# Second layer's entry: x times the norm's weights and root before the split, its input products on scaled fp16 parts

## The chip, the cores and the metric

The kernel runs on one core of one Trainium2 chip. The metric is device time in microseconds (us) of one execution; the runs of the kernel before took 2181.03, 2181.20 and 2181.38 us. The engines are TensorE (PE in the profile, its weight loads PEld), VectorE (DVE), ScalarE (ACT), GpSimd (POOL) and SyncE (SP); DMA transfers are issued from SP and POOL.

## The reference, cut to what matters

An encoder of two layers over 1024 tokens with 1024 channels. Each layer enters with

```
h = rmsnorm(x, g_mix[l]);  p = h @ w_in[l]
c_q  = rmsnorm(p[:, :384], g_q[l])        # -> q = c_q @ w_uq
c_kv = rmsnorm(p[:, 384:640], g_kv[l])    # -> k, v = c_kv @ w_ukv
k_rope = rope(p[:, 640:672])
a, gt = split(p[:, 672:])
u = silu(layernorm(dwconv31(a * sigmoid(gt))))
x = x + concat(attention(q, k, v), u) @ w_o[l]
h2 = rmsnorm(x, g_ffn[l]);  z = dwconv3(h2 @ w_up[l])
x = x + (silu(zg) * zv) @ w_down[l]
```

rmsnorm(x, g) is x · 1/sqrt(mean x² + 1e-6) · g. The output is the rmsnorm of the last x with g_final. All data are float32.

## The kernel before, in words

**Layout.** Channels lie on the 128 partitions, tokens along the free dimension: x is eight tiles of 128 x 1024, called x_0 to x_7. A float32 product is made of three products of parts: a tensor is split into an upper part ("h", rounded) and a lower part ("l", what the rounding left), and h·h, h·l and l·h are added in PSUM. Most products of the kernel use fp16 parts that have been scaled by a power of two so that they lie well in fp16's range. The products of w_in, in both layers, use parts of the type fp32r instead, which need no scaling.

**Blocks.** w_in comes in 13 blocks of 128 columns and one of 64: g0 to g3 (the gate gt), a0 to a3, kv0 and kv1, kr (k_rope), q0 to q2. One block's product, here called a section, is 8 channel tiles x 2 halves of the tokens x 3 products of parts, which is 48 matmuls of 128x512; kr is 32. Its result fills two PSUM banks as one 128x1024 tile (pg, pa, pkv, pkr, pq).

**Order.** Every engine has its own list of instructions, and runs it in the order in which the program writes it (`manual_schedule`); an instruction that has to wait holds up all that stand behind it on its engine. In the feed-forward part (`feed`, with `wo_steps`, `up_steps` and `down_steps`) the list is made by `put(step, rank, f)`: a step is one product on PE, and f is emitted with that step, sorted by rank. In `project` a clock of costs in the code spreads the work of the vector engines over the sections.

**The end of layer 1** (`down_steps`, loop l = 0). The down product runs in seven passes (`ORDER` 1, 5, 6, 3, 7, 2, 4) over 11 pairs of channel tiles. Its fp16 inputs are called ab (activations, split on ACT at L1540 and DVE at L1541) and wd (weights, fetched by SP, scaled and split on ACT at L1493 and DVE at L1494). After a pass `evict` adds its PSUM banks (pd) to four x tiles: L1456 on DVE. Pass 4 is the last. Its last three steps run bank by bank (m = 0 to 3), so that its banks for x_4, x_5, x_6 and x_7, second half of the tokens, close one after another; the four evictions of it finish x.

**The norm of layer 2.** `norm_sums` squares x on ACT (L258, xsq) and adds the squares on DVE (L263, L265, xss). `norm_root` transposes the sums on PE (L284, rx_0t and rx_512t, for the first and the second half of the tokens) and takes the root in eight small DVE instructions (L295 to L303). `norm_spread` brings the root to all partitions on PE (L322), and ACT copies it (L1720, rx). For half 0 all of this lies within pass 4. `norm_apply` (L1722) multiplies x by the norm's weights g_mix in two instructions for each x tile and half: ACT makes the upper part xs_h (L1732), DVE the lower part xs_l (L1733, three operands); it also stores raw x to DRAM (the residual, x_mid). The root is not in xs: it multiplies the results later.

**Entry to layer 2** (`next_sections`, L534). `resume` has POOL fetch the blocks g0, a0 and g1 as fp32r (L204); `complete` then negates each on ACT (L208) and has POOL fetch it a second time with an adding DMA (L209), so the lower part needs no DVE. PE runs the three sections for half 0 (L558, L564), then for half 1; the root's transposes for half 1 stand behind g0's half 1, and its spread behind a0's half 1.

**The rest of the products** (`project`, from L876 on). The sections a1 to q2 follow (L245, kr at L810), then the keys k0 to k3, and u, n and v, which belong to the queries and values. The evictions bring the root in: a gate takes three instructions (DVE L649, ACT sigmoid L650, DVE L652), its glu one on DVE (L657), a latent (kv and q) one on DVE (L679), then a square on ACT and its addition on DVE, the rotary key an ACT copy and two on DVE (L718 to L721). Between them DVE and POOL work off the taps of the 31-tap convolution (DVE L2039; ACT L2045 makes "far" ones, which a DMA adds in). `root` and `rooted` normalize the latents; the parts of the normalized ones, kvs and cqs, feed the keys and queries (L748 ACT, L750 DVE).

**Buffers.** Tiles come from rings: `wr` has 3 slots of 128x1024 float32 (raw weights, far taps), `ws` 8, `m` 8, and `b` 31 (`blk`).

Of the kernel before, what the change touches and what calls it, by code (L numbers as in the profile page):

```python
# [18 lines left out]
T = 1024  # L19
D = 1024  # L20
DEPTH = 2
# [102 lines left out]
WARM = 8  # L124

# [19 lines left out]
class Encoder:  # L145
# [45 lines left out]
    def cast(self, l, name, tag="ws"):  # L191
        src = self.weight_source(l, name)
        if name != "kr":
            return self.cast_tile(src, f"w{name}{l}", tag)
        w = self.tmp(tag, f"w{name}{l}", F32R, (128, 8, 128))
        hi, lo = w[:, :, 0:64], w[:, :, 64:128]
        src = src.rearrange("p (k m) -> p k m", k=8)
        self.nc.gpsimd.dma_start(out=hi, in_=src)
        return w, hi, lo, src

    def cast_tile(self, src, name, tag="ws"):
        hi, lo = (self.tmp(tag, name + i, F32R, tuple(src.shape)) for i in "hl")
        w = hi, lo
        self.nc.gpsimd.dma_start(out=hi, in_=src)  # L204
        return w, hi, lo, src

# [196 lines left out]
    def run(self):  # L403
        nc, a = self.nc, self.a
        self.par = [self.cp.tile([128, NPAR], F32, name="par0")]
        self.first = self.blk("first")
        nc.scalar.dma_start(out=self.first[:, 0:520], in_=a["x_first"])
        self.ones_r = self.cp.tile([128, 128], F32R, name="ones_r")
        self.ones = self.ones_r.bitcast(F32)
        self.ones_b = self.ones_r.bitcast(BF16)[:, 1::2]  # L410
        nc.vector.memset(self.ones, 1.0)
# [3 lines left out]
        self.xd = [a["x"], self.dp.tile([8, 128, T], F32, name="x_mid")]  # L415
        carry = None
# [117 lines left out]
    def next_sections(self, l, nxt, supply):  # L534
        names = ("g0", "a0", "g1")
        w = [self.complete(*e) for e in nxt["w"]]
        for k in range(8):
            self.norm_apply(l, nxt["x"], nxt, 1, k)
        self.norm_sums(l, nxt["x"], nxt, 1, range(4, 8))
        supply(-16.0)  # L540
        self.pp.tile([128, T], F32, name=f"skip{l}", tag="w1", bufs=1)
        ps = [self.wide(f"p{n}{l}") for n in names]
        for c in range(2):
# [23 lines left out]
    def project(self, l, carry):  # L567
# [13 lines left out]
        col = lambda i, n=1: qk[:, i:i + n]  # L581
        st = {}
# [64 lines left out]
        def gate(j):  # L647
            g = gates[j] = self.blk(f"gate{l}_{j}")
            nc.vector.tensor_tensor(out=g, in0=ps[f"g{j}"], in1=rx, op=ALU.mult)  # L649
            nc.scalar.activation(out=g, in_=g, func=AF.Sigmoid)  # L650
            yield 1.22, 1.5
            nc.vector.tensor_tensor(out=g, in0=g, in1=rx, op=ALU.mult)  # L652
            yield 1.22, 0.0

        def glu(j):
            g = u[j] = gates.pop(j)
            nc.vector.tensor_tensor(out=g, in0=ps[f"a{j}"], in1=g, op=ALU.mult)  # L657
# [19 lines left out]
        def latent(name, out, key, j):  # L677
            c = self.blk(f"c{name}{l}")
            nc.vector.tensor_tensor(out=c, in0=ps[name], in1=rx, op=ALU.mult)  # L679
            out.append(c)  # L680
            if j == 0:
                st[key] = self.blk(f"{key}{l}")
                nc.scalar.activation(out=st[key], in_=c, func=AF.Square)
                yield 1.22, 0.0
# [3 lines left out]
            yield 1.22, 1.5  # L688
# [26 lines left out]
        def key_rope():  # L715
            p, cos, sin = ps["kr"], st["cos"], st["sin"]
            t = self.blk(f"krt{l}")
            nc.scalar.copy(out=t[0:64, :], in_=p[64:128, :])  # L718
            yield 0.0, 1.5
            nc.vector.tensor_tensor(out=t[0:64, :], in0=p[0:64, :], in1=t[0:64, :], op=ALU.add)  # L720
            nc.vector.tensor_tensor(out=t[0:64, :], in0=t[0:64, :], in1=rx[0:64, :], op=ALU.mult)  # L721
# [91 lines left out]
        def inputs(name):  # L813
            return lambda: self.product(ps[name], self.tiled(w[name]), hl)
# [60 lines left out]

        def supply(now, turn=TURN):  # L876
# [3 lines left out]
            while turning and turning[0][1] <= now + turn:  # L880
                name, at, e = turning.pop(0)
                w[name] = self.complete(*e)
# [10 lines left out]
        for n, (name, weight, emit, evict, after) in enumerate(seq):  # L893
            supply(clock["pe"])
# [282 lines left out]
    def up_steps(self, l, steps, put):  # L1177
# [7 lines left out]
        self.ds = self.cp.tile([128, 2 * NF], F32, name=f"ds{l}", tag="ds", bufs=1)  # L1185
# [239 lines left out]
        for f in range(NF):  # L1425
# [14 lines left out]
            put(c + max(STORE_LAG, SQUARE_LAG.get(f, 1)), 3, lambda f=f: act_store(f))  # L1440
        for j in range(NF // 2):
# [8 lines left out]
    def down_steps(self, l, steps, put):  # L1450
        nc, a = self.nc, self.a
        base, last, half = len(steps), l == DEPTH - 1, NF // 2
        done, rest = HALVES
        act, x, casts, w, pairs, ps, nxt, sq, late_r, turns, st = {}, {}, {}, {}, {}, {}, {}, {}, {}, {}, {}
# [43 lines left out]
        def total():  # L1498
            st["ps"] = self.pp.tile([128, 2 * NF], F32, name=f"ds{l}p", tag="d4", bufs=1)
            nc.tensor.matmul(st["ps"], self.ones, self.ds[:, 0:2 * NF], start=True, stop=True)  # L1500

        def scales():
            f = self.ds[:, 0:16]
            cut = lambda i, n=1: f[:, i:i + n]
            nc.vector.tensor_reduce(out=cut(0, 2), in_=st.pop("ps").rearrange("p (e f) -> p e f", e=2), op=ALU.add, axis=AX.X)
# [7 lines left out]
            st["a"], st["w"], st["up"], st["back"], st["nback"] = (cut(i) for i in (4, 5, 8, 9, 10))  # L1513

# [54 lines left out]
        def evict(i, m):  # L1569
# [4 lines left out]
            else:  # L1574
                plus(xm, ps[BANK_SET[i], m], st["nback" if o else "back"])

# [26 lines left out]
        put(base + DOWN_TOTAL, 0.6, scales)  # L1603
        for m in range(4):
# [40 lines left out]
        put(end - 1, 6, resume)  # L1645
# [75 lines left out]

    def norm_apply(self, l, x, nxt, c, k, cs=None, r=None):  # L1722
# [3 lines left out]
        if l < DEPTH:  # L1726
            g = self.par[l][:, P_GMIX + k:P_GMIX + k + 1]
            if c == 0:
                nxt["hl"].append([self.tmp("m", f"xs{l}_{k}{i}", F32R) if k >= 4 else self.blk(f"xs{l}_{k}{i}", F32R)
                                  for i in "hl"])  # L1730
            hi, lo = (t[:, cs] for t in nxt["hl"][k])
            nc.scalar.activation(out=hi, in_=xk, func=AF.Copy, scale=g)  # L1732
            nc.vector.scalar_tensor_tensor(out=lo, in0=xk, scalar=g, in1=hi.bitcast(F32),  # L1733
                                           op0=ALU.mult, op1=ALU.subtract)
            nc.sync.dma_start(out=self.xd[l][k][:, cs], in_=xk)
# [45 lines left out]
    def attention(self, l, u, conv, away, spill, kvs, loaded, ahead, wo, begun):  # L1781
# [119 lines left out]
        def sums(h, main, st, y, rb):  # L1901
            pr = self.bank(f"sr{l}_{h}", (8, 128))
            nc.tensor.transpose(pr, st["sums"], self.ident)
            rs = self.cp.tile([8, 128], F32, name=f"rs{l}_{h}", tag="rs", bufs=2)
# [299 lines left out]
```

## Time and profile before

| | us |
|---|---|
| median of three runs | 2181.2 |
| profiled execution, span | 2179.0 |
| around the span (median less span) | 2.2 |
| PE busy | 2169.7 |
| DVE busy | 1844.7 |
| ACT busy | 1456.6 |
| POOL busy | 537.2 |

The profile is one execution, recorded by the hardware; its span runs from the first to the last instruction. Times in the rows are in us from the start of the span, durations in ns where they are whole numbers above 100. A row of the chain of waits says when a stretch of work began, how long it took, on which engine and line. An arrow shows out<-in, and x48 is a count. An instruction's duration reaches past the start of the next one on the same engine, so that in a row of equal instructions the distance of their starts is what each costs its engine: eight DVE instructions of 0.75 us in a row start 0.66 us apart.

The program enters layer 2's products at 1087.24 us and begins layer 2's last value products, which feed attention, at 1276.99 us.

### The profile page before, as it was taken

The numbers are of one execution on the slowest core, as the hardware profiler recorded it, in microseconds if no ns is written. First come the engines' busy times: TensorE is split into PE (matmuls) and PEld (weight loads), VectorE is DVE, ScalarE is ACT, GpSimd is POOL, SyncE is SP. The second block draws the span as 40 slices with busy tenths as digits, with TensorE's granted clock in tenths as the row PEclk, the third lists the DMA queues.
The fourth block names the chain that finished last, engine by engine and source line by source line (L and its number), as shares of the span: only waits on it lengthen the run. The fifth ranks groups of instructions, "written<-read, shape, count | busy, mean of one in ns | idle before, by whom it ended". The sixth has DMA issues, their size and how long they took to land.

```text
span 2179.0 us, 29766 instructions
## 1 busy us (share of the span) xinstructions
PE 2169.7 (100%) x10722; PEld 1260.7 (58%) x10722; DVE 1844.7 (85%) x2531; ACT 1456.6 (67%) x2183; POOL 537.2 (25%) x534
## 2 busy tenths in 40 slices
PE   9999999999999999999999999999999999999998
PEld 8887665754444444644488876667544444446445
DVE  6989999879998887887859789998898888878877
ACT  6455888746898886554623668886478888865544
POOL 1223777211111111000012355771112111110000
PEclk9999999999999999999999999999999999999999
DMA  6898878754688885554578986886646888856533
GB/s 195 184 187 212 164 152 171 245 163 104 149 244 259 222 261 145 193 178 151 166 177 164 188 207 134 159 186 200 175 100 164 261 241 242 241 141 218 182 111 122
DMA packets 163013, 400.96 MB, mean 184 GB/s; under 512 B 21888, under 2 KB 29936, under 8 KB 162864
## 3 DMA queue, kind: packets, MB, share of 16 engines
q0 software_dynamic: 62528, 145.89, 36.4%
q1 hardware_dynamic: 100048, 252.63, 33.8%
q8 instruction: 84, 1.38, 0.3%
q10 hardware_dynamic: 288, 0.53, 0.1%
q14 instruction: 65, 0.53, 0.1%
HBM read 270.75 MB, written 69.66 MB: 156 GB/s over the span
## 4 chain that ended last, share of the span: by engine, by line
PE 98%; ACT 1%; DVE 1%; issue 0%; DMA 0%; DVEq 0%; ACTq 0%
PE p L1306 36%; PE pd L1551 18%; PE po L1026 7%; PE s L1818 7%; PE t L1858 5%; PE pq L245 3%; PE pa L245 3%; PE o L1880 2%; PE pkv L245 2%; PE pg L245 2%; PE pg L564 2%; PE pn L245 2%; PE o L1885 1%; PE pv L1794 1%; PE pk L245 1%; PE pa L564 1%
## 5 line engine op out<-in xcount | busy, mean ns | idle before, releaser
L1306 PE MATMUL p<-b,w 128*128 128x512 f16 x3696 | 800.0, 379 | 0.2
L1306 PEld LDWEIGHTS <-w 128*128 128x128 f16 x3696 | 358.7, 98 | 431.9 <-issue 0.8
L1551 PE MATMUL pd<-ab,wd 128*128 128x512 f16 (+2 forms) x1920 | 404.2, 373 | 0.0
L1196 POOL DMA_DIRECT2D wu<-in_w_up x176 | 152.2, 879 | 770.2 <-DVE w L1270 581.5
L1551 PEld LDWEIGHTS <-wd 128*128 128x128 f16 x1656 | 161.9, 98 | 179.4 <-issue 0.5
L1818 PE MATMUL s<-k,q 96*128 96x512 f16 x768 | 186.9, 379 | 0.0
L1270 DVE SCALAR_TENSOR_TENSOR w<-wu,wf,w 128x512 f16<-128x512 f32 (+1 forms) x216 | 177.2, 834 | 3.6 <-ACT w L1267 3.6
L1861 DVE SCALAR_TENSOR_TENSOR pt<-t,pt 128x512 f16<-128x512 f32 x256 | 163.0, 676 | 10.0 <-ACT pt L1860 9.0
L1267 ACT ACTIVATE w<-wu,wf 128x512 f16<-128x512 f32 (+1 forms) x216 | 164.8, 781 | 0.1
L1860 ACT ACTIVATE pt<-t 128x512 f16<-128x512 f32 x256 | 139.1, 596 | 32.0 <-PE t L1858 30.0
L1820 DVE TENSOR_REDUCE mx<-s 128x1 f32<-128x1024 f32 x128 | 155.0, 1211 | 1.0 <-PE s L1818 1.0
L1540 ACT ACTIVATE ab<-ac,ds 128x512 f16<-128x512 f32 x108 | 75.5, 717 | 108.7 <-DVE ac L1455 73.0
L1828 ACT ACTIVATE p<-s,mx 128x1024 f32<-128x1024 f32 x128 | 143.3, 1120 | 2.2 <-DVE mx L1820 1.8
L2039 DVE SCALAR_TENSOR_TENSOR conv<-gate,par,conv 128x1009 f32<-128x1009 f32 (+14 forms) x110 | 139.9, 1274 | 3.1 <-ACT conv L659 0.4
L2056 POOL TENSOR_SCALAR late<-gate,par 128x1019 f32<-128x1019 f32 (+13 forms) x99 | 135.5, 1368 | 27.2 <-PE pn L245 13.9
L1858 PE MATMUL t<-ident,p 128*128 128x128 f32 x1024 | 136.6, 275 | 0.9 <-ACT p L1828 0.6
L1858 PEld LDWEIGHTS t<-ident,p 128*128 128x128 f32 x1024 | 116.8, 141 | 34.8 <-issue 7.4
L1766 DVE SCALAR_TENSOR_TENSOR o<-zg,par,o 128x1023 f32<-128x1023 f32 x88 | 112.7, 1281 | 8.9 <-ACT o L1760 7.4
L1314 DVE SCALAR_TENSOR_TENSOR zg<-p,wf,zg 128x512 f32<-128x512 f32 x72 | 54.0, 750 | 71.2 <-PE p L1306 61.6
L1766 DVE SCALAR_TENSOR_TENSOR v<-zv,par,v 128x1023 f32<-128x1023 f32 x88 | 112.1, 1276 | 0.0
L1818 PEld LDWEIGHTS <-q 96*128 96x128 f16 x768 | 74.0, 97 | 64.6 <-issue 2.1
L1541 DVE SCALAR_TENSOR_TENSOR ab<-ac,ds,ab 128x512 f16<-128x512 f32 x108 | 79.9, 748 | 19.2 <-ACT ab L1540 19.2
(2179 smaller groups left out, 3814.1 us busy)
## 6 DMA issues: line engine op xcount, KB each, us to landing
wu<-in_w_up SPq DMA_DIRECT2D x98, 512.0 KB
wu<-in_w_up POOLq DMA_DIRECT2D x176, 256.0 KB, 4.8
sd<-in_w_down SPq DMA_DIRECT2D x44, 512.0 KB
ws<-sd SPq DMA_DIRECT2D x44, 512.0 KB
act<-v SPq DMA_DIRECT2D x36, 512.0 KB
ac<-act SPq DMA_DIRECT2D x72, 256.0 KB
wo<-in_w_o POOLq DMA_DIRECT2D x32, 256.0 KB, 7.7
x_mix<-y SPq DMA_DIRECT2D x32, 256.0 KB
```

The costliest lines, as they stand in the source:

```text
L245: nc.tensor.matmul(ps[:, HALVES[c]], w, x[:, HALVES[c]], start=(k == 0 and s == 0), stop=(k == n - 1 and s == 2))
L1026: self.nc.tensor.matmul(ps, p[:, sl], q[:, cs], start=(k == 0 and t == 0), stop=(k == 3 and t == 2))
L1196: nc.gpsimd.dma_start(out=dst, in_=src, accum_op=ALU.add)
L1267: nc.scalar.activation(out=t, in_=src, func=AF.Copy, scale=scale[f])
L1270: nc.vector.scalar_tensor_tensor(out=t, in0=src, scalar=scale[f], in1=hi, op0=ALU.mult, op1=ALU.subtract)
L1306: nc.tensor.matmul(ps, w[p][:, k * 128:(k + 1) * 128], b[:, q], start=(i in (1, 5, 2) and k == 0 and t == 0), stop=(k == 3 and t == 2), sk ...
L1551: nc.tensor.matmul(ps[t, m][:, cs], w[i, j][p][:, m * 128:(m + 1) * 128], b[:, q, cs], start=(i in (1, 5, 2) and j == 0 and s == 0), stop= ...
L1766: self.nc.vector.scalar_tensor_tensor(out=o[:, a:b], in0=z[:, at + a:at + b], scalar=self.par[l][:, tap:tap + 1], in1=o[:, a:b], op0=ALU.m ...
L1818: nc.tensor.matmul(ps[:, cs], q[0:96, i, qs], k[0:96, j, cs], start=(s == 0), stop=(s == 2))
L1820: nc.vector.tensor_reduce(out=mx, in_=ps, op=ALU.max, axis=AX.X, negate=True)
L1858: nc.tensor.transpose(tp[:, i, qi * 128:(qi + 1) * 128], st["p"][2 * qp + qi][:, kt * 128:(kt + 1) * 128], self.ident)
L1861: nc.vector.scalar_tensor_tensor(out=lo, in0=tp, scalar=P_SCALE, in1=hi, op0=ALU.mult, op1=ALU.subtract)
```

## The change

**In the up stage of layer 1**: 14 blocks of layer 2's w_in are loaded by SP (`next_load`) and squared on ACT (`next_squares`), which also sums the squares; the squares' sum is only needed for a scale. `total` and `scales` in the down stage carry these sums along, and `next_scales` (seven small DVE instructions) makes powers of two out of them: one for the weights, one for x, one for the way back. They stand in a new tile `wz`.

**At the entry to layer 2**: each block is fetched once, raw, by SP into a `wr` slot (`cast`); ACT makes its scaled fp16 upper part (`scaled`) and DVE its lower part (`scaled_rest`, 128x1024). This holds for g0, a0 and g1 at the end of the down stage (`split_next`) and for the later blocks in `supply`.

**x**: `norm_apply` multiplies x in place by wz (g_mix and the scale) and the root on DVE (L1828), casts the upper part to fp16 on ACT (L1829), and DVE subtracts it for the lower part (L1817, one x tile later). x_mid is stored from `evict` instead. The root of the second half therefore has to be there before the second half is multiplied: its transposes now stand behind the fifth of g0's eight channel tiles of half 0, its spread behind the fifth of a0's, and `norm_apply` of half 1 follows.

**Evictions in layer 2**: the root is in x already, so a gate is one ACT sigmoid with a scale, the glu one DVE instruction with a scale, a latent one ACT instruction (L706), the rotary key's copy is scaled and one DVE instruction less. The ring `rs` of the attention's sums has one slot instead of two.

```diff
@@ next_sections
-        w = [self.complete(*e) for e in nxt["w"]]
-        for k in range(8):
-            self.norm_apply(l, nxt["x"], nxt, 1, k)
-        self.norm_sums(l, nxt["x"], nxt, 1, range(4, 8))
-        supply(-16.0)
+        supply(-30.0)
+        w = [e[0] for e in nxt["ready"]]
+        self.norm_sums(l, nxt["x"], nxt, 1, (7,))
...
-                if (c, i) == (0, 0):
-                    self.upper_first(ps[i], self.tiled(w[i]), nxt["hl"], HALVES[c])
-                for k in range(8 if c or i else 0):
-                    self.partial(ps[i], self.tiled(w[i]), nxt["hl"], k, (c,))
-                if c == 1 and i == 0:
-                    self.norm_root(l, nxt, 1, self.bank)
-                if c == 1 and i == 1:
-                    self.norm_spread(l, nxt, 1, self.bank)
-        return nxt["hl"], nxt["r"], dict(zip(names, ps))
+                for k in range(8):
+                    self.partial(ps[i], tiles[i], nxt["hl"], k, (c,))
+                    if (c, i, k) == (0, 0, 4):
+                        self.norm_root(l, nxt, 1, self.bank)
+                    if (c, i, k) == (0, 1, 4):
+                        self.norm_spread(l, nxt, 1, self.bank)
+                        for m in range(8):
+                            self.norm_apply(l, nxt["x"], nxt, 1, m)
+        supply(-16.0)
+        return nxt["hl"], None, dict(zip(names, ps))
@@ scaled, scaled_rest
+        nc.scalar.activation(out=hi, in_=src, func=AF.Copy, scale=self.wz[:, 12:13])
...
+        self.nc.vector.scalar_tensor_tensor(out=lo, in0=src, scalar=self.wz[:, 12:13], in1=hi, op0=ALU.mult, op1=ALU.subtract)
@@ latent
-            nc.vector.tensor_tensor(out=c, in0=ps[name], in1=rx, op=ALU.mult)
+            if l:
+                nc.scalar.activation(out=c, in_=ps[name], func=AF.Copy, scale=by)
+            else:
+                nc.vector.tensor_tensor(out=c, in0=ps[name], in1=rx, op=ALU.mult)
@@ supply
+                if l and name in BLOCKS:
+                    e = self.scaled(*e)
+                    w[name] = e[0]
+                    launch(rest_of(e), st.get("n", -3) - 2)
+                    continue
@@ up_steps
+            for n in range(len(BLOCKS)):
+                m = at[NEXT_SQUARES] + 3 * n // 2
+                put(m - 6, 5.6, lambda n=n: next_load(n))
+                put(m, 2.7, lambda n=n: next_squares(n))
@@ down_steps
+            put(base + DOWN_TOTAL + 12, 6, next_scales)
+            for m in range(3):
+                put(at[4, tail] + m + 1, 1.5, lambda m=m: sums(1, (4 + m,)))
...
-                nxt["w"] = [self.cast(l + 1, n) for n in ("g0", "a0", "g1")]
+                nxt["raw"] = [self.cast(l + 1, n) for n in ("g0", "a0", "g1")]
...
+        put(end - 8, 6, resume)
+        for i in range(0 if last else 3):
+            put(end - 4 + i, 3.2, lambda i=i: split_next(i))
+            put(end - 3 + i, 3.6, lambda i=i: self.scaled_rest(*nxt["ready"][i]))
@@ norm_apply, l < DEPTH
-            nc.scalar.activation(out=hi, in_=xk, func=AF.Copy, scale=g)
-            nc.vector.scalar_tensor_tensor(out=lo, in0=xk, scalar=g, in1=hi.bitcast(F32),
-                                           op0=ALU.mult, op1=ALU.subtract)
-            nc.sync.dma_start(out=self.xd[l][k][:, cs], in_=xk)
+            nc.vector.scalar_tensor_tensor(out=xk, in0=xk, scalar=self.wz[:, k:k + 1], in1=nxt["r"][:, cs], op0=ALU.mult, op1=ALU.mult)
+            nc.scalar.copy(out=hi, in_=xk)
+            self.norm_rest(nxt)
+            nxt["late"] = lo, xk, hi
+            if k == 7:
+                self.norm_rest(nxt)
```

The rows of order below name instructions as the two programs have them: the line, the operation, out<-in and the shape. L1522 in them is the eviction (L1456 before), L282 the addition of squares (L265), L301 the transposes (L284), L312 the root's first instruction (L295), L222 `scaled_rest`.

More of the change, by code (lines that the diff above doesn't have):

```diff
@@ L192, in cast @@
         src = self.weight_source(l, name)
+        if l and name in BLOCKS:
+            raw = self.tmp("wr", f"w{name}{l}r")[:, 0:src.shape[-1]]
+            self.nc.sync.dma_start(out=raw, in_=src)
+            return name, raw
         if name != "kr":
@@ L1513, in scales, with next_scales @@
             st["a"], st["w"], st["up"], st["back"], st["nback"] = (cut(i) for i in (4, 5, 8, 9, 10))
+        def next_scales():
+            self.half_exponent(z(10, 2), z(8, 2))
+            self.power(z(8), z(10), -1.0, 198.0)
+            self.power(z(12), z(11), -1.0, 204.0)
+            self.power(z(13), z(10), 1.0, 56.0)
+            self.power(z(14), z(11), 1.0, 50.0)
+            nc.vector.tensor_tensor(out=z(13), in0=z(13), in1=z(14), op=ALU.mult)
+            nc.vector.tensor_scalar(out=z(0, 8), in0=self.par[l + 1][:, P_GMIX:P_GMIX + 8], scalar1=z(8), scalar2=None, op0=ALU.mult)
         def rescale(m):
@@ L1575, in evict @@
                 plus(xm, ps[BANK_SET[i], m], st["nback" if o else "back"])
+            if not last and i in (3, 7, 2, 4):
+                nc.sync.dma_start(out=self.xd[l + 1][o + m][:, cs], in_=xm)
         order = [(i, j) for i in ORDER for j in range(half)]
@@ L1603, in down_steps @@
         put(base + DOWN_TOTAL, 0.6, scales)
+        if not last:
+            put(base + DOWN_TOTAL + 12, 6, next_scales)
+            for m in range(3):
+                put(at[4, tail] + m + 1, 1.5, lambda m=m: sums(1, (4 + m,)))
         for m in range(4):
@@ L1720, in norm_spread, with norm_rest @@
         self.nc.scalar.copy(out=nxt["r"][:, cs], in_=ps)
+    def norm_rest(self, nxt):
+        if "late" in nxt:
+            lo, xk, hi = nxt.pop("late")
+            self.nc.vector.tensor_tensor(out=lo, in0=xk, in1=hi, op=ALU.subtract)
     def norm_apply(self, l, x, nxt, c, k, cs=None, r=None):
```

81 lines of the change are left out of this document (65 added, 16 removed).

## The prediction

> **What bounds the kernel now.** I read the page's busy times and its chain first, then the chain of waits around layer 2's entry, then the busy time by stretches.
>
> ```profile
> PE 2169.7 (100%) x10722; PEld 1260.7 (58%) x10722; DVE 1844.7 (85%) x2531; ACT 1456.6 (67%) x2183; POOL 537.2 (25%) x534
> ...
> PE 98%; ACT 1%; DVE 1%; issue 0%; DMA 0%; DVEq 0%; ACTq 0%
> ```
>
> PE is busy nearly all of the 2179.0 us span. So what the change can win is PE time alone, and what it can lose is any wait that it gives PE. The chain of waits at the place of the change:
>
> ```profile
> 1069.11 18.13 PE pd L1551 x84
> 1087.24 5.46 PE pg L558 x24
> ...
> 1109.03 0.44 PE rx_512t L284 x4
> ...
> 1114.95 0.44 PE rx_512s L322 x4
> ...
> 1120.88 10.88 PE pa L245 x48
> ...
> 1197.04 7.25 PE pkr L810 x32
> ...
> 1226.94 0.45 PE rkv1s L322 x4
> ...
> 1239.51 8.16 PE pk L245 x36
> 1247.67 0.87 PE rq1t L284 x8
> ```
>
> The rows follow each other without a gap: PE goes from layer 1's last product (pd) to layer 2's sections and on to the keys (pk). An fp16 matmul takes 18.13 / 84 = 0.216 us, an fp32r one 10.88 / 48 = 0.2267 us (kr: 7.25 / 32, the same).
>
> ```profile
> 831.00:881.00 50.00, 50.00 (x235) 22.70 (x233) 36.09 (x45) 33.57 (x48) 5.24 (x6) 1.00 0.53 132
> ...
> 1142.00:1175.00 33.00, 33.00 (x147) 27.32 (x146) 31.87 (x27) 11.12 (x11) 9.02 (x11) 1.00 0.64 122
> 1175.00:1204.00 29.00, 29.00 (x130) 24.01 (x129) 28.32 (x24) 12.99 (x14) 8.68 (x12) 1.00 0.97 197
> ```
>
> After the span, the columns of these stretches are the busy time of PE, PEld, DVE, ACT and POOL, then the granted clock (1.00). DVE is the runner-up: 31.87 + 28.32 = 60.19 of 62 us from 1142 to 1204. Whatever DVE gets late there stays late.
>
> **The change part by part.** *Faster matmuls.* 13 sections of 48 and one of 32 are 656 matmuls, each shorter by 0.2267 - 0.216 = 0.0107 us: 7.0 us at most, of which 144 matmuls (1.5 us) lie in g0, a0 and g1 and 512 (5.5 us) after them.
>
> *The entry.* What DVE has to do between layer 1's last parts and the root, in these rows of before:
>
> ```profile
> 1072.04 1.28 DVE L1494 SCALAR_TENSOR_TENSOR wd<-wd_48r,ds,wd 128x1024 f16<-128x1024 f32 x1 [0.23 <-ACT wd L1493]
> 1073.24 0.75 DVE L1494 SCALAR_TENSOR_TENSOR wd<-wd_410r,ds,wd 128x512 f16<-128x512 f32 x1
> 1073.90 0.75 DVE L1733 SCALAR_TENSOR_TENSOR xs_0l<-x,par,xs_0h 128x512 fp32r<-128x512 f32 x1
> ...
> 1081.45 0.75 DVE L1456 SCALAR_TENSOR_TENSOR x<-pd,ds,x 128x512 f32<-128x512 f32 x1 [0.18 <-PE pd L1551]
> ...
> 1087.28 0.75 DVE L1456 SCALAR_TENSOR_TENSOR x<-pd,ds,x 128x512 f32<-128x512 f32 x1 [1.19 <-PE pd L1551]
> ...
> 1093.25 3.08 DVE L265 TENSOR_TENSOR xss<-xss,xsq 128x512 f32<-128x512 f32 x4
> 1109.50 0.69 DVE L295 TENSOR_REDUCE rx_512v<-rx_512t 128x4 f32<-128x512 f32 x1 [13.18 <-PE rx_512t L284]
> ...
> 1111.42 0.16 DVE L300 SCALAR_TENSOR_TENSOR rx_512y<-rx_512q,rx_512y 128x4 f32<-128x4 f32 x1
> ```
>
> By starts, a 128x1024 instruction occupies DVE for 1.20 us (1072.04 to 1073.24) and a 128x512 one for 0.66. Before, the last addition ends at 1096.3 and PE asks for it at 1109.03: 12.7 us to spare. The change spends this twice. In DVE's list before, around x_4's eviction:
>
> ```order
> L1733 SCALAR_TENSOR_TENSOR xs_6l<-x_6_8467,par_154,xs_6h 128x512
> L1456 SCALAR_TENSOR_TENSOR x_4_8419<-pd_10_8122,ds_4021,x_4_8419 128x512
> L1733 SCALAR_TENSOR_TENSOR xs_7l<-x_7_8490,par_154,xs_7h 128x512
> L1456 SCALAR_TENSOR_TENSOR x_5_8445<-pd_11_8126,ds_4021,x_5_8445 128x512
> L1456 SCALAR_TENSOR_TENSOR x_6_8467<-pd_12_8130,ds_4021,x_6_8467 128x512
> L1456 SCALAR_TENSOR_TENSOR x_7_8490<-pd_13_8134,ds_4021,x_7_8490 128x512
> ```
>
> The evictions follow as PE closes the banks. The list now, from the same eviction to the root:
>
> ```order
> L1522 SCALAR_TENSOR_TENSOR x_4_8479<-pd_10_8180,ds_4022,x_4_8479 128x512
> L282 TENSOR_TENSOR xss_9145<-xss_9145,xsq_5124_9795 128x512
> L222 SCALAR_TENSOR_TENSOR wa0s<-wa01r,wz,wa0s 128x1024
> L1828 SCALAR_TENSOR_TENSOR x_7_8550<-x_7_8550,wz,rx_9663 128x512
> L1817 TENSOR_TENSOR xs_6_9780<-x_6_8527,xs_6_9780 128x512
> L1817 TENSOR_TENSOR xs_7_9801<-x_7_8550,xs_7_9801 128x512
> L1522 SCALAR_TENSOR_TENSOR x_5_8505<-pd_11_8184,ds_4022,x_5_8505 128x512
> L282 TENSOR_TENSOR xss_9145<-xss_9145,xsq_5125_9817 128x512
> L222 SCALAR_TENSOR_TENSOR wg1s<-wg11r,wz,wg1s 128x1024
> L1522 SCALAR_TENSOR_TENSOR x_6_8527<-pd_12_8188,ds_4022,x_6_8527 128x512
> L1522 SCALAR_TENSOR_TENSOR x_7_8550<-pd_13_8192,ds_4022,x_7_8550 128x512
> L282 TENSOR_TENSOR xss_9145<-xss_9145,xsq_5126_9834 128x512
> ```
>
> Two weight parts and three x instructions now stand between the evictions, and x_7's square and addition come after all of them. On PE the root's transposes moved up:
>
> ```order
> L582 MATMUL pg_9853<-xs_4_9760,wg0s 128x512
> L582 LDWEIGHTS wg0s
> L582 MATMUL pg_9853<-xs_4_9760,wg0s 128x512
> L301 MATMUL rx_512t<-ident,xss_9145 128x128 x4
> L582 LDWEIGHTS wg0s
> L582 MATMUL pg_9853<-xs_5_9764,wg0s 128x512
> ```
>
> They stand 15 matmuls into g0, where 96 fp32r matmuls (half 0 of all three sections and half 1 of g0) came before them until now. From 1073.90 on DVE has ahead of the last addition: 8 multiplications of x, 4 lower parts ab, 4 evictions (16 x 0.66 = 10.6; the x multiplication is the form of the last row group below, 744 ns), 8 subtractions and 4 additions (12 x 0.63 = 7.6, for 687 ns less the same overlap), 3 weight parts (3 x 1.20 = 3.6): 21.8 us, so 1095.7 if DVE never waits.
>
> ```profile
> L1752 ACT CAST ab<-ac 128x512 fp32r<-128x512 f32 x22 | 13.4, 610 | 0.0
> L1754 DVE TENSOR_TENSOR ab<-ac,ab 128x512 fp32r<-128x512 f32 x22 | 15.1, 687 | 4.7 <-ACT ab L1752 4.7
> L1740 DVE SCALAR_TENSOR_TENSOR x<-x,gfin,rx 128x512 f32<-128x512 f32 x8 | 5.5, 744 | 0.0
> ```
>
> It will wait: at five places (x_0's cast, two ab parts, the squares of x_4 and x_5) its next instruction needs a 610 to 710 ns ACT instruction that begins only when DVE's last one ends, 0.65 each: 3.3 us, so 1099.0. PE, 15 x 0.216 = 3.2 us after 1087.24, is there at 1090.5. It waits 5.2 to 8.5 us; I take 8.5, since the ACT steps between are in the list. The smaller waits before (x_4's eviction now comes late for g0's bank) are part of it. The rest of the entry has its cover: the root's eight instructions (1109.50 to 1111.58: 2.1 us) end before PE reaches the spread, 24 matmuls on; then DVE needs 8 x 1.3 us for half 1, from 1106 to 1117, and PE uses the last of these tiles at about 1117. So a1 starts at 1087.24 + 144 x 0.216 + 0.9 (transposes and spread) + 8.5 = 1127.7, against 1120.88: **+6.9**.
>
> *The clock.* All stretches above show 1.00, but there PE never pauses. The only rows of PE after a rest are the warm-up's at the start:
>
> ```profile
> L435 PE MATMUL warm<-ones_r 128*128 128x128 f32 x16 | 3.7, 426 | 1.1 <-DVE ones_r L411 1.1
> L1858 PE MATMUL t<-ident,p 128*128 128x128 f32 x1024 | 136.6, 275 | 0.9 <-ACT p L1828 0.6
> ```
>
> The same shape takes 3.7 / 16 = 0.231 us there and 136.6 / 1024 = 0.133 later, so 3.7 us after a rest are worth 2.1: 1.6 us lost. Whether a wait of 8 us counts as a rest no row shows: 0 to 1.6. I take 1.6, the only row of PE after idling: **+1.6**.
>
> [...]
>
> *The sections after it.*
>
> ```profile
> L1370 ACT ACTIVATE dsq<-sd 128x1024 f16<-128x1024 f32 x44 | 45.9, 1044 | 0.0
> ...
> L652 DVE TENSOR_TENSOR gate<-gate,rx 128x1024 f32<-128x1024 f32 x8 | 9.8, 1222 | 7.5 <-ACT gate L650 7.5
> L649 DVE TENSOR_TENSOR gate<-pg,rx 128x1024 f32<-128x1024 f32 x8 | 9.8, 1220 | 9.2 <-ACT rx L1720 4.5 <-PE pg L564 4.2 <-PE pg L245 0.6
> ...
> L679 DVE TENSOR_TENSOR cq<-pq,rx 128x1024 f32<-128x1024 f32 x6 | 7.2, 1208 | 0.0
> ```
>
> DVE loses two instructions of 1.22 us per gate and one of 1.21 per latent, and gains a weight part of 1.28 per block; this is about even, so from 1142 on it stays as late as it starts. ACT gains an eviction of about 1.0 us (the krt copy's size, below) per latent, five in all. The rows of ACT, and two of DVE, that lead to the keys:
>
> ```profile
> 1204.53 1.01 ACT L718 COPY krt<-pkr 64x1024 f32<-64x1024 f32 x1
> ...
> 1215.79 1.06 ACT L729 ACTIVATE krt<-krt 32x1024 f32<-32x1024 f32 x1 [2.70 <-DVE krt L728]
> ...
> 1223.94 1.14 ACT L748 ACTIVATE cqs_0h<-cq,par 128x1024 fp32r<-128x1024 f32 x1
> 1227.47 1.07 ACT L695 COPY rkv<-rkv1s 128x512 f32<-128x512 f32 x2 [2.40 <-PE rkv1s L322]
> ...
> 1241.83 1.14 ACT L748 ACTIVATE cqs_2h<-cq,par 128x1024 fp32r<-128x1024 f32 x1
> ```
>
> ```profile
> 1235.99 1.26 DVE L750 SCALAR_TENSOR_TENSOR kvs_0l<-ckv,par,kvs_0h 128x1024 fp32r<-128x1024 f32 x1
> ```
>
> The squares of krt (1215.79) hang on DVE, so they come 6.9 later, at 1222.7. From them to the end of cqs_0h ACT is solid for 9.3 us; with cq0's eviction 10.3: 1233.0. PE's spread ends at 1227.4 + 6.9 - 464 x 0.0107 = 1229.3, so rkv's copies start 3.7 late. From that copy to kvs_0l's end before: 9.8 us, now 1242.8; PE needs it 4 matmuls into k0, at 1239.51 + 0.9 + 6.9 - 5.5 = 1241.8: **+1.0**. ACT then has two more evictions ahead of the last q latent's square; the root of q (rq1t, before at 1247.67, now 1250.1) waits for its addition, which DVE reaches at the square's end, 1249 + 1.2, or a key's part later, 1253: 0 to 2.9, I take **+1.9**, nearer the upper end, because the key's part stands first in the list.
>
> *Under cover.* 14 squares of 1.04 us (dsq's row above) and their loads lie in the up stage, where ACT has 50 - 33.57 = 16.4 us of 50 free: 14.6 fit; 0, and if their clumps delay a PSUM eviction up to +2. The fetches by POOL and their additions fall away, on a queue that nothing here waits for. `next_scales` is seven small instructions (0.16 us at 1111.42) in the down stage; x_mid's stores only leave their place.
>
> *Sum*, against the profiled span: 2179.0 + 6.9 - 5.5 + 1.0 + 1.9 + 1.6 = 2184.9, and with the 2.2 us around it (median 2181.2) 2187.1. I call it **2187.0**.
>
> **The rivals.** *A, DVE keeps ahead:* the sums are ready at PE's 1090.5 and the whole 7.0 comes in: 2174.2. Against it stand 21.8 us of DVE work for 16.6 us of PE; for it only that the order could hide less waiting than I count. It is the not-slower side in its pure form; even the bound without DVE's waits gives 5.2 - 7.0: 2179.4. *B, the entry waits, the rest recovers:* 6.9 - 5.5 = +1.4: 2182.6, within what can be told; it decides if ACT gets through its list to kvs and the last q latent 3 us sooner than I count, with the clock kept. *C, more queues:* the raw weights share three slots with the far taps; a load that starts only when DVE has made the part before it delays ACT's upper parts, and squares in the up stage delay evictions: 3 to 5 us over the sum, 2190 to 2192.
>
> **How the numbers follow.** 0.2% (4.4 us) is what a measurement here can tell from no change, so same is 2176.8 to 2185.6. Forecast with or without the clock term (2185.5 to 2187.1): 0.50, of which 0.10 lies under the line. B and the gentle end of A (2179 to 2183): 0.24, all same. A in full, 2174: 0.06. C: 0.20. So faster 0.06, same 0.34, slower 0.60. The range reaches from A's gentle end, 2179.4, to C's lower half, 2191: it leaves out A in full and the rest of C.
>
> **What would show it.** Right: PE waits 5 to 9 us at rx_512t for DVE's xss, with DVE solid from 1074; a1 starts 5 to 9 us later; matmuls of the sections at 0.216; waits of 1 to 2 us before k0 and at rq1t; a lower granted clock right behind the long wait. Wrong: no wait at rx_512t, or fp16 sections that take 10.9 us, or PE waits in the up stage.

## The result and the profile after

The changed kernel takes 2195.32 us (median of five runs, 2193.89 to 2195.74), the kernel before 2181.38 in the same comparison: a ratio of 1.0062, 95% interval 1.0051 to 1.0073. It is 13.9 us slower. The forecast of 2187.0 stood for 5.8 us, so the direction was right and the size less than half of what came. The profiled execution's span went from 2179.0 to 2192.1 us; it was the fastest of the five (2193.89 us), so about 1.4 us of the median do not show in the trace.

The page's busy times after the change:

```profile
PE 2167.3 (99%) x10722; PEld 1202.8 (55%) x10722; DVE 1855.7 (85%) x2556; ACT 1478.2 (67%) x2218; POOL 516.5 (24%) x506
```

PE is busy only 2.4 us less than before, although its fp16 sections are shorter by 7.0 us; a slow clock took part of that back (1.7 us at the entry and 1.7 us in q2, below). The rest is waiting, nearly all of it in three places. PE's part of the table of waits (line, what released it, total, times, longest):

```profile
PE kt L622 <- ACT rkv L724: 6.3, 2, 6.0
PE pg L582 <- DVE x L1522: 5.8, 1, 5.8
PE rkv1s L339 <- DVE rkv1y L317: 3.6, 1, 3.6
```

The first place is the entry, on PE:

```profile
1094.20 5.05 PE L582 MATMUL pg<-xs,wg0s 128*128 128x512 f16 x15 [5.84 <-DVE x L1522]
1099.70 0.66 PE L301 MATMUL rx_512t<-ident,xss 128*128 128x128 f32 x4 [0.45 <-DVE xss L282]
1100.19 2.11 PE L582 MATMUL pg<-xs,wg0s 128*128 128x512 f16 x9
...
1128.47 10.52 PE L262 MATMUL pa<-xs,wa1s 128*128 128x512 f16 x48
```

and on DVE in the same stretch:

```profile
1090.12 1.28 DVE L222 SCALAR_TENSOR_TENSOR wa0s<-wa01r,wz,wa0s 128x1024 f16<-128x1024 f32 x1
1091.31 0.75 DVE L1828 SCALAR_TENSOR_TENSOR x<-x,wz,rx 128x512 f32<-128x512 f32 x1
1091.97 1.51 DVE L1817 TENSOR_TENSOR xs<-x,xs 128x512 f16<-128x512 f32 x2
1093.40 0.74 DVE L1522 SCALAR_TENSOR_TENSOR x<-pd,ds,x 128x512 f32<-128x512 f32 x1
...
1098.16 1.49 DVE L282 TENSOR_TENSOR xss<-xss,xsq 128x512 f32<-128x512 f32 x2
```

PE did not get as far as the root's transposes before it waited. g0's PSUM tile takes two banks, those of x_4 and x_5, and x_5's eviction stands behind a0's weight part, x_7 and two subtractions: it runs at 1093.40 instead of 1083.39, and g0 starts right after it. Before, this eviction stood ten us earlier, and waited only for PE:

```profile
1083.39 0.75 DVE L1456 SCALAR_TENSOR_TENSOR x<-pd,ds,x 128x512 f32<-128x512 f32 x1 [0.53 <-PE pd L1551]
```

g0's first 15 matmuls then take 5.05 us; at a granted clock of 1.00 (1102 to 1106) a0's first 15 take 3.40, and so do these in experiment 2. The last addition ends at 1099.65, PE waits 0.45 more for it, and a1 starts 7.6 us late (1128.47 against 1120.88). The granted clock of the stretches from 1094 (the column before the last two):

```profile
1094.00:1097.00 3.00, 2.80 (x7) 0.99 (x7) 2.24 (x4) 0.63 (x1) 0.00 (x0) 0.50 0.23 87
1097.00:1100.00 3.00, 2.55 (x12) 1.04 (x11) 2.50 (x4) 1.26 (x2) 0.00 (x0) 0.90 0.71 194
1100.00:1104.00 4.00, 4.00 (x22) 1.95 (x21) 1.83 (x8) 0.00 (x0) 0.00 (x0) 1.00 0.90 338
```

The second and third place lie in the sections after it. PE there, and the keys:

```profile
1233.30 1.17 PE L339 MATMUL rkv1s<-ident,rkv1y 128*128 128x128 f32 x8 [3.64 <-DVE rkv1y L317]
1240.45 0.59 PE L622 MATMUL kt<-qk,ones_r 128*128 128x3 f32 x2 [5.98 <-ACT rkv L724]
1240.90 12.21 PE L262 MATMUL pq<-xs,wq2s 128*128 128x512 f16 x48
```

```profile
1253.11 8.18 PE pk L262 x36
```

The keys begin 13.6 us late (1239.51 before). From a1 to here the sections saved 5.5 us; the waits took 3.6 and 6.0, and q2 took 1.7 more than the other sections' 10.36 (its start to the next, 12.07 us in the chain): 7.6 - 5.5 + 9.6 + 1.7 = 13.4. The granted clock was below 1 again while q2 began (0.50 and 0.71):

```profile
1240.00:1242.00 2.00, 1.55 (x5) 0.86 (x6) 1.86 (x7) 2.00 (x4) 0.07 (x1) 0.50 1.08 214
1242.00:1246.00 4.00, 4.00 (x14) 1.58 (x13) 2.57 (x5) 3.77 (x5) 2.01 (x2) 0.71 1.06 206
```

The tile kt is a small product that stands ahead of q2 in PE's list. Its data come from ACT's squares and are ready by 1232.5; it waits for rkv's copy on ACT because the kernel keeps two single PSUM banks here, rkv1s fills both, and the copy frees the first. What made the copies late stands further up in ACT's list:

```profile
1193.38 1.15 ACT L2143 ACTIVATE far<-gate,par 128x1023 f32<-128x1023 f32 x1 [6.24 <-DMA conv<-far]
...
1206.82 1.15 ACT L2143 ACTIVATE far<-gate,par 128x1023 f32<-128x1023 f32 x1 [9.17 <-DMA conv<-far]
...
1219.47 1.15 ACT L2143 ACTIVATE far<-gate,par 128x1022 f32<-128x1022 f32 x1 [3.89 <-DMA conv<-far]
1220.64 1.11 ACT L748 ACTIVATE krt<-pkr,wz 64x1024 f32<-64x1024 f32 x1
...
1229.38 1.05 ACT L763 ACTIVATE krt<-krt 32x1024 f32<-32x1024 f32 x1 [2.71 <-DVE krt L762]
...
1239.84 1.05 ACT L724 COPY rkv<-rkv1s 128x512 f32<-128x512 f32 x2
```

ACT stands before the far taps of the convolution, each time until the adding DMA of an earlier far tap has landed. krt's copy, which had nothing to do with them, stands behind them in ACT's list: 1220.64 instead of 1204.53, of which 3.6 us are PE's own lateness (kr's product ends at 1207.9 instead of 1204.3). For the far taps of both layers, the view adds up what ACT and POOL together waited for (first line) and ACT's part of it (second line), after and then before:

```profile
  DMA conv<-far: 33.0, 8
...
  ACT far L2143: 26.7, 7
```

```profile
  DMA conv<-far: 11.9, 3
...
  ACT far L2045: 1.0, 1
```

Before, nearly all of this was POOL's own waiting; ACT's list stopped for 1.0 us. Now it stops for 26.7.

### The profile page after: what moved, and what is told of

It reads as the page before. It is cut to its first block, busy times and chain, and to the rows that moved or that the text cites. A ratio compares the mean times of both kernels' runs of the same rounds, so it can differ in the third digit from the quotient of the medians.

```text
span 2192.1 us, 29801 instructions
## 1 busy us (share of the span) xinstructions
PE 2167.3 (99%) x10722; PEld 1202.8 (55%) x10722; DVE 1855.7 (85%) x2556; ACT 1478.2 (67%) x2218; POOL 516.5 (24%) x506
## 5 line engine op out<-in xcount | busy, mean ns | idle before, releaser
L2144 POOL DMA_DIRECT2D conv<-far x31 | 26.5, 855 | 367.7 <-ACT far L2143 349.1
```

## The experiments

Two theories stood at the start. **Shared slots**: the raw weights now rotate through the same three wr slots as the far taps. A slot comes free for a far tap only when DVE has made the weight part before it (ACT waited 0.3 and 1.7 us for two of them), or an adding DMA has landed (26.7 us), and ACT's list stops there. **Queue of DVE**, the prediction's reading: the entry made DVE late, DVE has no room to recover, and ACT's five evictions come on top.

**1. Slots of their own.**

```diff
-            raw = self.tmp("wr", f"w{name}{l}r")[:, 0:src.shape[-1]]
+            raw = self.tmp("wr" if name in BLOCKS[:3] else "ws", f"w{name}{l}r", F32, (128, T))[:, 0:src.shape[-1]]
```

> The raw weights of the eleven blocks from a1 on take slots of the ring ws (eight slots, of which each block used two before the change and uses one after it) and no longer the three slots of wr, which the far taps use. Theory 'shared slots': in the changed kernel ACT stands before the far taps for 5 to 9 us at a time until an adding DMA or a lower part gives a slot free, so the rotary key and the root of kv come late and PE waits 3.6 us at rkv1s and 6.0 us at kt and loses some 1.7 us of clock in q2; without the sharing these go, and what is left are the waits at the entry and 1 to 3 us before the keys: 2185 to 2188 us. Rival 'queue of DVE' (the entry made DVE 7.6 us late, and it stays so, with ACT's five evictions on top): ACT's idle time before the far taps is only slack, the waits at rkv1s and kt stay above 6 us in all, 2192 to 2195 us.

Measured: 2184.57 us, ratio 1.0015 (1.0005 to 1.0024), 10.7 us less than the changed kernel by the medians. The far taps' waits for DMAs fell to

```profile
  DMA conv<-far: 8.7, 3
...
  ACT far L2143: 1.6, 2
```

krt's copy and rkv's copies came earlier on ACT,

```profile
1208.95 1.11 ACT L748 ACTIVATE krt<-pkr,wz 64x1024 f32<-64x1024 f32 x1
...
1231.65 1.05 ACT L724 COPY rkv<-rkv1s 128x512 f32<-128x512 f32 x2
```

and on PE rkv1s no longer waited, kt only 1.4 us:

```profile
1229.83 1.04 PE L339 MATMUL rkv1s<-ident,rkv1y 128*128 128x128 f32 x8
1232.26 0.38 PE L622 MATMUL kt<-qk,ones_r 128*128 128x3 f32 x2 [1.40 <-ACT rkv L724]
1232.51 10.52 PE L262 MATMUL pq<-xs,wq2s 128*128 128x512 f16 x48
```

q2's row is back at 10.52 us from 12.21. The entry is unchanged (a1 at 1128.81), and the keys start at 1242.67 instead of 1252.76, so DVE's lateness at the entry was not what held them. The theory of the shared slots is shown, for the larger part of the loss.

**2. PE kept busy at the entry.** 24 matmuls that nothing reads, ahead of g0.

```diff
+        idle = self.bank("idle")
+        for _ in range(24):
+            self.nc.tensor.matmul(idle, w[0][:, 0, 0], nxt["hl"][0][0][:, HALVES[0]], start=True, stop=True)
```

> 24 more matmuls into an unused bank stand on PE between layer 1's last product and g0, from parts that are ready there; nothing reads them. They fill 5.2 of the 5.8 us that PE waits there. Theory 'clock': g0's first 15 matmuls took 5.05 us because PE had rested, and take 3.3 now; a1 starts 1.8 us earlier (1126.7 instead of 1128.5), the granted clock stays at 1.00 there. Rival 'late operands': the 15 matmuls wait for operands that the profile does not show, 5.05 us stays. What reaches the end is 0 to 1.8 us, since the later waits hang on DVE and the far taps: 2193.5 to 2195.3 us.

Measured: 2193.57 us, ratio 1.0056 (1.0039 to 1.0072).

```profile
1088.63 5.34 PE L562 MATMUL idle<-xs,wg0s 128*128 128x512 f16 x24
1094.63 3.40 PE L585 MATMUL pg<-xs,wg0s 128*128 128x512 f16 x15 [0.66 <-DVE x L1525]
1100.13 0.66 PE L301 MATMUL rx_512t<-ident,xss 128*128 128x128 f32 x4 [2.09 <-DVE xss L282]
```

The 15 matmuls take 3.40 us instead of 5.05, the time of 15 at a granted clock of 1.00: it was the clock (0.50 from 1094 to 1097 in the changed kernel), and behind a rest of only 0.66 us they ran at full pace. But the time came back as a wait at rx_512t (2.09 instead of 0.45), since DVE's last addition ends when it ended. a1 starts at 1128.90; counted from rx_0t's transposes, which lie ahead of the entry, that is 65.1 us in both kernels. At the entry of the changed kernel the slow clock cost nothing. The median lies 1.8 us under the changed kernel's, with overlapping intervals; the profiled spans are equal (2192.2 and 2192.1), so nothing in the trace accounts for it.

**3. No squares in the up stage.** Loads and squares of the 14 blocks are left out, the sums set by one memset.

```diff
-                put(m - 6, 5.6, lambda n=n: next_load(n))
-                put(m, 2.7, lambda n=n: next_squares(n))
+            put(2, 9.1, lambda: nc.vector.memset(self.ds[:, 2 * NF + 1:2 * NF + 1 + len(BLOCKS)], 1.0))
```

> The 14 loads and 14 squares in the up stage are left out; the sums are set to 1.0 per partition and block, about what these weights give, so the scale is the same or a neighbouring power of two. Up to layer 1's down stage the changed kernel is 0.47 us late. Theory: that is the squares' work on ACT in the up stage, and it goes; the rest stays, 2194.8 us. Rival: the squares and their 7 MB cost more than the chain shows, by late evictions in several places: 2191 to 2193 us.

Measured: 2194.33 us, ratio 1.0060 (1.0045 to 1.0075); no difference from the changed kernel that the intervals can tell. The waits at the entry, rkv1s and kt are as in the changed kernel (5.8, 3.5, 5.8 us). From rf_1t's transposes in layer 1's up stage to rx_0t's, PE took 570.6 us before (492.3 to 1062.9), 571.0 in the changed kernel (492.4 to 1063.4) and 570.6 here (493.3 to 1063.9). In experiment 1, which has the squares, it took 570.9 to 571.0 (from 492.8). So the squares cost 0.3 to 0.4 us, about what the theory had, and no more. (What lies ahead of that ended at 492.3 to 493.3 in these four executions.)

**4. The latents back on DVE**, with slots of their own.

```diff
-                nc.scalar.activation(out=c, in_=ps[name], func=AF.Copy, scale=by)
+                nc.vector.tensor_scalar(out=c, in0=ps[name], scalar1=by, scalar2=None, op0=ALU.mult)
```

> As the first kernel, and the five latents are evicted on DVE, as before the change, instead of ACT. Theory 'shared slots' with ACT's five evictions as the next in line: the waits before the keys get shorter than in the first kernel, by 1 to 3 us. Rival 'queue of DVE': DVE has no room for five more instructions of 1.2 us, the root of kv and the keys come later, 1 to 4 us above the first kernel.

Measured: 2186.27 us, ratio 1.0024 (1.0014 to 1.0033), 1.7 us above experiment 1; the two kernels' runs don't overlap (from 2185.62 up, to 2185.01). kt waits 2.64 us instead of 1.40. That is the rival's forecast: DVE has no room for five more instructions, and the move of the latents to ACT, which the prediction had put among the costs, is a gain where the slots are apart.

**5. Two weight parts later in DVE's list**, with slots of their own.

```diff
         self.norm_sums(l, nxt["x"], nxt, 1, (7,))
+        self.scaled_rest(*nxt["ready"][1])
...
                         self.norm_root(l, nxt, 1, self.bank)
+                        self.scaled_rest(*nxt["ready"][2])
```

> As the first kernel (raw weights in slots of their own), and of the three weight parts that DVE makes at the entry, a0's stands behind the last addition of squares and g1's behind the root. Theory 'place in DVE's queue': PE's wait at the entry is made of what stands ahead of the evictions and of the last addition, so 2.4 us go of the addition (it ended at 1099.65 in the changed kernel) and 1.2 us of x_5's eviction; a1 starts some 2.4 us earlier than in the first kernel (1126.4 instead of 1128.8), and as DVE and ACT are then earlier too, it reaches the end: 2182 us. Rival 'the rest of the entry': a0's and g1's products then wait for their lower parts instead, or the keys' chain takes it up, 2184 us.

Measured: 2183.26 us, ratio 1.0008 (0.9999 to 1.0017), 1.3 us under experiment 1; half of what was expected (2182).

```profile
1093.94 5.08 PE L584 MATMUL pg<-xs,wg0s 128*128 128x512 f16 x15 [4.64 <-DVE x L1524]
1098.86 0.60 PE L301 MATMUL rx_512t<-ident,xss 128*128 128x128 f32 x4
...
1127.57 10.52 PE L262 MATMUL pa<-xs,wa1s 128*128 128x512 f16 x48
```

Counted from the end of layer 1's product in each trace (1088.71 in experiment 1, 1089.30 here), x_5's eviction let PE go 1.2 us earlier, as worked out, and PE's wait at rx_512t (0.79 in experiment 1) is gone. But now the 15 slow matmuls (5.08 us) set the end of the stretch. With the 2.4 us that were worked out for it the last addition ends at about 1098.2, an estimate (experiment 1's transposes start at 1100.03, right behind it); here the transposes start at 1098.86, 0.7 us later, and at 3.40 us the 15 would have ended before it. So some 0.6 us of the clock's 1.7, all of them free in the changed kernel, are paid here, and a1 comes 1.8 us earlier and not 2.4. Another part of what is missing lies ahead of the entry: the profiled execution reached the end of layer 1's product 0.6 us later than experiment 1's.

**6. Channel tiles in the outer loop**, with slots of their own. x_4 to x_7 are evicted and their squares added ahead of x_3 to x_7 of half 0, and the three weight parts are made one step earlier.

```diff
+        self.norm_sums(l, nxt["x"], nxt, 1, (6,))
+        self.norm_apply(l, nxt["x"], nxt, 0, 3)
         self.norm_sums(l, nxt["x"], nxt, 1, (7,))
+        for m in range(4, 8):
+            self.norm_apply(l, nxt["x"], nxt, 0, m)
...
+        for k in range(8):
+            for i in (0, 2, 1):
+                self.partial(ps[i], tiles[i], nxt["hl"], k, (0,))
+            if k == 3:
+                self.norm_root(l, nxt, 1, self.bank)
+            if k == 5:
+                self.norm_spread(l, nxt, 1, self.bank)
+                for m in range(8):
+                    self.norm_apply(l, nxt["x"], nxt, 1, m)
+        for i, k in [(i, k) for k in range(4) for i in range(3)] + [(i, k) for i in range(3) for k in range(4, 8)]:
+            self.partial(ps[i], tiles[i], nxt["hl"], k, (1,))
```

> As the first kernel, with another order at the entry: PE goes through the channel tiles in the outer loop and g0, g1, a0 in the inner one (for half 1 in the first four tiles), so it uses a tile every 1.95 us instead of 0.65; DVE evicts x_4 to x_7 and adds their squares ahead of x_3 to x_7 of half 0; the root's transposes stand behind four tiles, its spread behind six. Theory 'place in DVE's queue': DVE's work is the same 21.8 us, but only what PE needs next stands first, so the waits of 6.6 us go but for about 0.5; a1 starts at 1120 to 1121.5 (1120.88 before the change, 1128.8 in the first kernel), the saved matmul time arrives in part: 2175 to 2178 us. Rival 'too much work': DVE has more to do than the stretch holds in any order, PE waits 3 us or more in other places: 2180 to 2184 us.

Measured: 2177.12 us, ratio 0.9981 (0.9972 to 0.9989). It is faster than both kernels, by 18.2 us than the changed one and by 4.3 us (0.2%) than the one before.

```profile
PE kt L627 <- ACT rkv L729: 1.7, 2, 1.4
...
PE pa L587 <- DVE x L1527: 0.6, 1, 0.6
PE rq1t L301 <- DVE qss L282: 0.5, 1, 0.5
```

```profile
1090.59 0.81 PE L587 MATMUL pa<-xs,wa0s 128*128 128x512 f16 x3 [0.59 <-DVE x L1527]
...
1097.06 0.60 PE L301 MATMUL rx_512t<-ident,xss 128*128 128x128 f32 x4
...
1121.53 10.52 PE L262 MATMUL pa<-xs,wa1s 128*128 128x512 f16 x48
```

With the same instructions in another order PE waits 0.6 us at the entry instead of 6.3 (6.6 in experiment 1), and the rows behind that wait run at full pace (three matmuls in 0.65 us). DVE's 21.8 us did not have to be done before the root: only what PE asks for next has to stand first.

**7. The same order, slots shared again**: the edit of experiment 6 without that of experiment 1.

> The order of the sixth kernel's entry, but the raw weights back in the three shared slots, as in the changed kernel. Theory: entry and slots are two separate costs, the entry gives 6 to 8 us here too: 2187 to 2189 us. Rival: the far taps and loads run at the pace of their three slots whenever the entry ends, so the waits before q1 and q2 grow by what the entry saves: 2192 to 2195 us.

Measured: 2187.31 us, ratio 1.0026 (1.0016 to 1.0035). The two costs are separate: the order is worth 8.0 us with shared slots and 7.5 without, the slots 10.7 with the old order and 10.2 with the new one. The waits at rkv1s and kt stay (3.7 and 5.2 us).

**8. PE kept busy before q2**, in the changed kernel: idle(n) issues n matmuls into q2's bank.

```diff
-        ... lambda: (start(keys_norm()), key_scale()))
+        ... lambda: (idle(16), start(keys_norm()), idle(26), key_scale()))
```

> The changed kernel, with 16 more matmuls on PE ahead of rkv1s and 26 ahead of kt, into q2's bank before its product begins; nothing reads them. They fill 3.4 of the 3.6 us and 5.6 of the 6.0 us that PE waits there. In the changed kernel q2 took 12.07 us instead of 10.36, at a granted clock under 1. Theory 'clock': PE had rested there as at the entry, q2 takes 10.4 us now and, as nothing that comes later waits for long, 1.7 us reach the end: 2193 to 2194 us. Rival 'hidden again': as at the entry (where filling the wait gave the 1.8 us back and the next wait took them), the keys wait for kvs or qss by as much, 2194.5 to 2195.5 us.

Measured: 2192.24 us, ratio 1.0052 (1.0038 to 1.0066).

```profile
1240.44 0.38 PE L622 MATMUL kt<-qk,ones_r 128*128 128x3 f32 x2 [0.48 <-ACT rkv L724]
1240.68 10.52 PE L262 MATMUL pq<-xs,wq2s 128*128 128x512 f16 x48
```

kt runs when it ran (1240.45), q2 takes 1.7 us less, and the span is 1.6 us shorter. By the medians it is 3.1 us, more than expected, but the intervals overlap. By the traces, one execution of each, the clock cost is real here, because nothing that comes after waits for long (rq1t 0.16 us).

**9. q0 later on ACT**, on top of experiment 6.

```diff
-        ... lambda: query_latent(0), lambda: root("kss", "kroot", KVL, "rkv"))
+        ... lambda: iter(()) if l else query_latent(0), lambda: root("kss", "kroot", KVL, "rkv"))
-        ... lambda: (start(keys_norm()), key_scale()))
+        ... lambda: (start(keys_norm()), key_scale(), l and launch(query_latent(0), len(seq))))
```

> The sixth kernel (own slots, channel tiles in the outer loop), and q0's eviction, square and split on ACT stand behind the copies of kv's root and the split of kv, instead of ahead of them. Theory 'ACT's new evictions in the queue': the last wait at kt (1.4 us, for rkv) comes from the 3.1 us that q0 takes on ACT just before; it goes, the wait at rq1t (0.5) stays or grows a little: 2175 to 2176.5 us. Rival 'just moved': ACT has the same work before q's root, so rq1t waits longer by what kt gains: 2177 us.

Measured: 2180.85 us, ratio 0.9997 (0.9989 to 1.0006): 3.7 us above experiment 6, and neither theory. kt's wait went (0.24), but the latents' evictions now come after the keys need their banks. k0 waits 0.7 us for the first, and k2:

```profile
1242.87 0.74 PE L262 MATMUL pk<-kvs_0h,wk1h 128*128 128x512 f32 x2 [1.89 <-ACT cq L711]
...
1244.84 1.05 PE L262 MATMUL pk<-kvs_1h,wk1h 128*128 128x512 f32 x2
```

k2's product waited 1.89 us for the last of them, and then ran at a granted clock of 0.60 from 1244 to 1248 (two matmuls start 0.85 us apart instead of 0.46). An eviction on ACT also frees a PSUM bank, and the expectation had only counted ACT's time.

## Why the prediction was wrong

The direction and, in size, the entry held; the sections after it did not.

**The bound, the saving.** PE is the bound, and the fp16 sections take 10.36 us instead of 10.88, as worked out.

**The entry, +6.9 and the clock, +1.6.** Together 8.5 forecast, 7.6 measured, of which 0.5 is older than the entry (0.3 to 0.4 from the squares). The sum of DVE's list was right: the last addition was put at 1099.0 and ended at 1099.65. Two things in it were off. The wait stood at g0's start, since g0's tile needs x_5's bank as well as x_4's, and only 0.45 us of it at rx_512t. And the clock term was added to a wait that ends at a fixed time: it is real (5.05 us for 15 matmuls, 3.40 in experiment 2), but it lay inside the stretch that DVE's last addition ends. It should have been a maximum, not a sum. The warm-up's rows, the term's source, show no lower clock (before's profile gives 1.00 from 1 to 5 us); the changed kernel's trace does: behind a rest of 5.84 us the granted clock was 0.50 from 1094 to 1097, 0.90 from 1097 to 1100 and 1.00 from 1100.

**The sections after it, +1.0 and +1.9.** This step failed. Its first half took krt's square from before's row and moved it by the entry's 6.9 us, to 1222.7; it ran at 1229.38. From there the forecast held: 10.3 us of ACT work to rkv's copies, put at 1233.0 from 1222.7, and measured 1229.38 to 1239.84, 10.5 us. What was missed are the 6.7 us ahead of it: "from 1142 on it stays as late as it starts" looked at the amount of work on DVE and ACT, and not at the slots that the moved weights take. ACT stands before the far taps for their DMAs 26.7 us instead of 1.0, and its whole list stops with them. Experiment 1 removes that and with it 10.7 us. The wait has a second cost, 1.7 us of slow clock in q2 (experiment 8).

The step also had the wrong place. It let PE feel rkv's late copies only through kvs, four matmuls into k0. But kt, ahead of q2 on PE, already waits for the first copy: before, it started at 1228.11, right behind that copy's end (1227.47 + 0.59). By the prediction's own times, copies 3.7 us late, kt would have waited about 3.7 us, and the waits at k0 and rq1t would have shrunk to next to nothing; that is about 1 us more than the step's 2.9, an estimate. In the changed kernel no PE wait stands at k0 or rq1t, and 9.6 us stand at rkv1s and kt.

In experiment 1, PE waits 1.4 us at kt, none at k0 and 0.7 at rq1t, 2.1 in all where the step had 2.9. krt's square runs there at 1221.19 and not at 1222.7. So without the shared slots the step's size is nearly right, but its places and times are not; that 2184.57 lies near the forecast without the clock term, 2185.5, is in part luck.

**Rival C** named the mechanism, with 3 to 5 us over the sum and a chance of 0.20. Its first half, the slots, was the case that came, at 8.3 us over the sum; its second half, squares that delay evictions in the up stage, was not (0.3 to 0.4 us). The prediction showed no working for its 3 to 5 us. A wr slot that a far tap takes is busy until its DMA has landed (4.5 to 13.5 us from issue to landing, median 7.1, over both layers), and eleven more tiles had to pass through the same three slots in the time of layer 2's 16 far taps; no run here shows whether such a count would have given the size.

**Rival A** (no wait) and B (the rest recovers) did not come. But the argument against A, 21.8 us of DVE work for 16.6 us of PE, was too strong: experiment 6 has the same work and a wait of 0.6 us at the entry. There the order decided, not the amount.

**Under cover.** The squares of the up stage cost 0.3 to 0.4 us (experiment 3), within the 0 to 2 that the prediction gave them; `next_scales` and x_mid's stores show in no wait of PE. ACT's evictions of the latents, booked as a cost, are better where they are (experiment 4, with slots apart).

## What to carry to other kernels

When a change moves a transfer to another ring of buffers, list who else rotates through that ring and what frees each slot: here ACT, with its list in order, waited 26.7 us for slots on behalf of everything that stood behind the far taps, and the cost appeared on PE at rkv1s and kt (3.6 and 6.0 us), which have no part in it. When an engine has more work than a stretch holds, ask which part is needed first before concluding that its consumer must wait; the same instructions in another order took the entry's wait from 6.3 to 0.6 us. The slow clock after a wait cost in these runs only what the next wait, if that ended at a time of its own, did not hide: nothing at the changed kernel's entry (experiment 2), some 0.6 of 1.7 us in experiment 5, 1.7 us in q2 (experiment 8).

## What was not expected of the hardware

The clock fell after rests of quite different length. In the changed kernel a rest of 5.84 us was followed by 0.50 from 1094 to 1097. In experiment 4 a rest of 2.64 us before kt was followed by no fall: q2 took 10.52 us from 1233.72, and the clock was 1.00 from 1230 to 1238.

```profile
1234.00:1238.00 4.00, 4.00 (x20) 1.79 (x19) 2.30 (x10) 3.97 (x6) 1.20 (x1) 1.00 1.10 207
```

In experiment 9 a rest of 1.89 us before k2, in a stretch in which PE had waited 0.7 us some 7 us before, was followed by a fall that began only a microsecond after PE had resumed at 1242.87 (matmuls 0.85 us per two from 1243.99):

```profile
1242.00:1244.00 2.00, 1.13 (x5) 0.88 (x6) 0.00 (x0) 1.97 (x3) 0.27 (x1) 0.95 0.41 49
1244.00:1248.00 4.00, 4.00 (x14) 2.88 (x13) 3.06 (x3) 4.00 (x5) 1.02 (x1) 0.60 0.70 173
```

So the length of a rest alone did not decide it: the clock fell after 1.89 us and not after 2.64. What else did, no run here settles.
